# Rotating keys in the stage that makes them, rotating queries straight from PSUM, and four value sums on VectorE

## The chip, the cores and the metric

The kernel runs on one core of a Trainium2 chip. The metric is device time in microseconds (us) for one execution of the whole program; lower is better. In the core, TensorE (PE) multiplies matrices and writes its sums to PSUM banks, VectorE (DVE), ScalarE (ACT) and GpSimd (POOL) work element by element on tiles of 128 partitions, and SyncE (SP) issues most of the DMA transfers. Each engine works through its own instructions in order and waits on semaphores for the others.

## The reference

One sub-layer of an encoder over 1024 tokens of width 1024, in float32. After a root-mean-square norm, one wide projection feeds three mixers: a dilated sliding-window attention ("a", three groups of eight heads of 64, dilations 1, 4 and 16), a grouped-query attention ("b"), and a cross-attention into 256 memory tokens ("m"). Each is gated, projected, and merged by sigmoid gates; an output projection and a norm close it. The change concerns mixer a alone:

```python
def rope(x, pos):
    ang = pos[:, None] * inv[None, :]
    x1, x2 = x[..., :half], x[..., half:]
    return concatenate([x1 * cos - x2 * sin, x1 * sin + x2 * cos], axis=-1)
...
h = rms_norm(x, g_pre)
a_qkv, bq, bk, bv, mq, ga, gb, gm, mg = split(h @ w_in, split_at, axis=-1)
aq = rope(a_qkv[:, :, 0], pos)
ak = rope(a_qkv[:, :, 1], pos)
av = a_qkv[:, :, 2]
for gi, (window, dil) in enumerate(A_GROUPS):
    o_g, lse_g = dilated_window_attention(aq[:, :, hs], ak[:, :, hs], av[:, :, hs], window, dil)
```

A head's rotation needs each feature times a cosine, plus its partner (32 features away in the head of 64) times a sine.

## The kernel before

All of it is one program of some 7,500 matmuls. Activations lie transposed: features on partitions, tokens along the free axis. A float32 product is done as three passes of a faster type: `split` (L105 on ScalarE, L106 on VectorE) cuts an operand into a high part and the rest, and each product is high by high, rest by high, high by rest. A unit of the projection has 128 features; its two halves of 512 tokens take 24 matmuls each into one PSUM bank `d` (L143, L145, L147), and two such banks alternate.

Four stages matter here. The times are those of the profiled execution.

- **Values' stage**, 460 to 598 us. The values of mixer a, and other products of this stage, are computed by a Strassen-Winograd scheme in the order of `PRODUCTS`: A11, A12, S2, S3, S4, S1, A22. `sum_at` forms the weight sums S1 to S4 (all on POOL, L897), `split_at` splits them, `v_out` (L909) adds the last product of a result to what has been kept in `vv` or `vy` and writes it to a tile `vr` (four buffers), and `v_store` scales it on ScalarE and stores it to `vdr`. Beside this `operand` scales the heads of mixer b (tiles `vot`, `vgt`, `vrt`, one buffer each) and stores them back.
- **Keys' stage**, 598 to 714 us. Six blocks `n` of seven products `i`, each product 12 matmuls into a bank `s`. POOL forms four sums in a block (`k_sum`, L978), `k_block` splits them into a tile `ch` (five buffers), and `k_evac` brings a finished product out: into the running sums `kv0` and `kv1` (L1012), or, added to these, into a tile `kr` (`k_out`, L999), which a DMA from ScalarE's queue stores to `kd`. The keys lie in `kd` unrotated, 128 features by 1024 tokens for each of 12 pairs of heads and group.
- **Windowed attention**, 714 to 1106 us. Twelve items (a pair of heads `p_` and a group `g`). `weave` mixes the matmuls of the next query units (`add_a`) on TensorE with the pieces of the attention: scores (L1279, from `aq` and `ak`), the softmax (`soft`: L1291 on VectorE with exponentials on ScalarE, L1292), transposes (L1318), and the products with the values (L1335). Each half of a query unit ends in `q_rope`, and each item's keys are fetched two items ahead by `k_fetch` (step T = 0 of an item) and rotated by `k_rope` (step T = 5).
- From 1106 us on, the merge gates' weights, the branch products and the output projection; the change doesn't touch them.

`q_rope` in the kernel before: VectorE multiplies the bank `d` by the sine table `tab1` into `t3a` (L1182, one buffer) and by the cosine table `tab0` into `t1a` (L1183, two buffers); four DMAs on SP's queue (`swapped`, L1176) move the 32-row quarters of `t3a` to their partners' rows in `t2a`; POOL adds `t1a` and `t2a` into `aq` (L1185), in the order that the group's dilation wants. For the keys, one DMA loads `kraw` from `kd` (L1202), four load `kswp` with quarters exchanged (L1176 too), VectorE multiplies each by a table (L1207, L1208), and POOL subtracts (L1212). The tables are loaded in the second block of the keys' stage and multiplied by the norm's factor `rb` in the third.

In the values' and keys' stages the order on every engine is that of the code. In the attention TensorE's order comes from the costs that `weave` counts; a scheduler sets that of the other engines, except for the first two items' keys, which are again in code order.

Of the kernel before, what the change touches and what calls it, by code (L numbers as in the profile page):

```python
# [15 lines left out]
S = 1024  # L16
# [34 lines left out]
def block(ctx: ExitStack, tc: tile.TileContext, x, xT, memT, cst, msk, bcst, tabA, gpost,  # L51
# [182 lines left out]
    kd = dram.tile([12, P, S], F32, name="kd")  # L234
# [659 lines left out]
    def sum_at(nm, k):  # L894
        a, b, op = {"S1": ("A21", "A22", OP.add), "S3": ("A11", "A21", OP.subtract),
                    "S2": ("S1", "A11", OP.subtract), "S4": ("A12", "S2", OP.subtract)}[nm]
        G.tensor_tensor(VR[nm][:, k], VR[a][:, k], VR[b][:, k], op=op)  # L897
# [9 lines left out]
    def v_out(u, t, j, ps_, z):  # L907
        r = vr()
        V.tensor_tensor(r, ps_, z, op=OP.add)  # L909
# [20 lines left out]
    def operand(r, stage):  # L930
        k, t = r // 2, half[r % 2]
        if stage == 0:
            OT[r] = [vb.tile([P, 512], F32, name=x) for x in ("vot", "vgt", "vrt")]
            nc.sync.dma_start(OT[r][0], od[1, k, :, t])
            nc.sync.dma_start(OT[r][1], g2d[1, k, :, t])
            for h in range(2):
                nc.sync.dma_start(OT[r][2][h * 64:h * 64 + 64], rld[2 * k + h:2 * k + h + 1, t].to_broadcast([64, 512]))
        elif stage == 1:
            ot, gt, rt = OT[r]
            V.scalar_tensor_tensor(ot, ot, 0.5, gt, op0=OP.mult, op1=OP.mult)  # L940
            V.tensor_tensor(ot, ot, rt, op=OP.mult)
        else:
            nc.sync.dma_start(od[1, k, :, t], OT.pop(r)[0])
# [42 lines left out]
    def k_block(n, nm):  # L986
        t = kp.tile([P, 1024], R, name="ch", bufs=5)
# [9 lines left out]
    def k_out(n, u, t, ps_, z):  # L997
        r = kp.tile([P, 512], F32, name="kr", bufs=4)
        V.tensor_tensor(r, ps_, z, op=OP.add)  # L999
        return lambda: nc.scalar.dma_start(kd[2 * n + u, :, half[t]], r)  # L1000

    def k_evac(n, i, ps_):
        nm = PRODUCTS[i][0]
        if nm == "A11":
            return [lambda: A.activation(kv_[0], ps_, AF.Copy)]
        if nm == "A12":
            return [k_out(n, 0, 0, ps_, kv_[0])]
        if nm == "A22":
            return [k_out(n, 1, 0, ps_, kv_[1])]
        if nm == "S1":  # L1010
            return [k_out(n, 1, 1, ps_, kv_[1]), k_out(n, 0, 1, ps_, kv_[0])]
        V.tensor_tensor(kv_[nm == "S3"], ps_, kv_[0], op=OP.add)  # L1012
        return []
# [4 lines left out]
    for n, (i, e, k) in enumerate(steps_v):  # L1018
# [12 lines left out]
        m = n + 2  # L1031
        if m < CLASSIC:
# [13 lines left out]
        for nm, s0 in (("S1", 2), ("S2", 2), ("S3", 7), ("S4", 11)):  # L1046
# [39 lines left out]
    kv_ = [kp.tile([P, 512], F32, name=f"kv{j}") for j in range(2)]  # L1086
    k_sum(0, 3)
# [3 lines left out]
    for n in range(6):  # L1091
        for i, (an, bn) in enumerate(PRODUCTS):
# [7 lines left out]
            behind = left.pop(0)() if left else []  # L1100
            if i == 0:
                k_block(n, "A22")
# [29 lines left out]
            if n == 1 and i == 3:  # L1132
                for j in range(2):
                    nc.sync.dma_start(tab[j], tabA[:, j])
# [5 lines left out]
            left.append(lambda n=n, i=i, b=dst: k_evac(n, i, b))  # L1140
    for f in left.pop(0)():
        f()
# [10 lines left out]
    with tc.tile_pool(name="aa", bufs=1, reuse_waits="tile") as aa:  # L1153
# [19 lines left out]
        def swapped(dst, src):  # L1173

            for a in range(4):
                nc.sync.dma_start(dst[32 * a:32 * a + 32], src[32 * (a ^ 1):32 * (a ^ 1) + 32])  # L1176

        def q_rope(o, half, p, g):

            t = slice(half * 512, half * 512 + 512)  # L1180
            t1, t2, u = [(ab if j == 1 else aa).tile([P, 512], F32, name=f"t{j}a", bufs=2 if j < 3 else 1) for j in (1, 2, 3)]
            V.scalar_tensor_tensor(u, p, -0.125, tab[1][:, t], op0=OP.mult, op1=OP.mult)  # L1182
            fp["last"] = V.scalar_tensor_tensor(t1, p, -0.125, tab[0][:, t], op0=OP.mult, op1=OP.mult)  # L1183
            swapped(t2, u)
# [14 lines left out]
        def k_fetch(p_, g):  # L1199

            KK[p_, g] = [ab.tile([P, S], F32, name=x) for x in ("kraw", "kswp")]
# [3 lines left out]
        def k_rope(p_, g):  # L1205
            kr, ks = KK.pop((p_, g))
            V.tensor_tensor(kr, kr, tab[0], op=OP.mult)  # L1207
            V.tensor_tensor(ks, ks, tab[1], op=OP.mult)  # L1208
            ka = OPS.setdefault((p_, g), {})["k"] = ab.tile([P, S], F32, name="ak", bufs=2)
            for x in range(2):  # L1210
                t = half[x]
                G.tensor_tensor(half_of(ka, x, g), classes(kr[:, t], g), classes(ks[:, t], g), op=OP.subtract)  # L1212
# [172 lines left out]
        def plan(it, pre, nxt):  # L1385
# [18 lines left out]
            def keys(key, T):  # L1404
                if T == 0:
                    k_fetch(*key)
                else:
                    with tc.issue_after(fp["last"].ins):
                        k_rope(*key)
# [7 lines left out]
            for T in range(NT if it else 4):  # L1417
# [7 lines left out]
                if it and it["ahead"] and T in (0, 5):  # L1425
# [115 lines left out]
        def first_keys():  # L1541
            yield 300.0
            k_rope(*seq[0])
            k_fetch(*seq[1])
            yield 400.0
            k_rope(*seq[1])
# [478 lines left out]
```

## Time and profile before

| | before |
|---|---|
| three runs, us | 1549.29, 1545.55, 1548.0 (median 1548.0) |
| profiled execution, us | 1544.46 |
| its span, us | 1542.7 |
| mean granted TensorE clock | 0.971 |
| busy, PE | 1431.0 us, 93% |
| busy, DVE | 937.8 us, 61% |
| busy, ACT | 655.8 us, 43% |
| busy, POOL | 532.1 us, 34% |

How to read it: the profile shows one execution. The span runs from its first instruction to its last, and the device time counts 1.8 us around it. An engine's busy time is the sum over its instructions, so it says little by itself: an engine can be busy for 61% of the span and still hold up another at one place. The granted clock is the share of TensorE's full rate that the chip allowed. A row of a stage gives the time from and to, its length, then busy time and number of instructions of each engine, the clock, the DMA engines' mean busy share, and GB/s. In a row of waits, "A <- B" means that A waited for B, followed by the total in us, the number of waits and the longest. In rows in order of time, the first number is the start in us, the second the duration, and brackets give the wait just before it and what ended it. "L143" is line 143 of the kernel printed above.

### The profile page before, as it was taken

Reading aid. Unit: us, or ns where it says so; the run is one execution under the profiler, and the core shown is the slowest. Engines: PE = TensorE matmul, PEld = TensorE weight load, DVE = VectorE, ACT = ScalarE, POOL = GpSimd, SP = SyncE. Lnnn points to the kernel's source line nnn. Section 1 sums busy time; section 2 is a strip of 40 time slices with the busy share of each in tenths; the row PEclk is TensorE's granted clock in tenths of the full one; section 3 lists DMA queues with packets and bytes.
Section 4 is the critical chain, followed back from the end, with each engine's and each line's share of the span. In section 5 each row is a group of like instructions: output and inputs, shape, how many; then the busy total and the mean of one; then the engine's idle time right before and its main releaser. Section 6 shows DMA issues by size and latency. Waiting matters only on the chain.

```text
span 1542.7 us, 21224 instructions
## 1 busy us (share of the span) xinstructions
PE 1431.0 (93%) x7556; PEld 1144.9 (74%) x7556; DVE 937.8 (61%) x1637; ACT 655.8 (43%) x1407; POOL 532.1 (34%) x406
## 2 busy tenths in 40 slices
PE   7999999999998989998698677787999999999998
PEld 7899876666666868887576565666887788888887
DVE  7755477767636746553434435554478878658743
ACT  6633456656553344221255353545543434222221
POOL 1325307666666003330323332331133333024322
PEclk9999999999999999999899798989999999999999
DMA  6322122222107694334344344433444443757132
GB/s 237 107 86 69 35 89 69 85 90 80 58 23 231 203 279 142 132 117 152 90 119 114 93 128 126 129 87 127 129 140 131 156 165 130 272 190 271 66 110 96
DMA packets 114139, 198.69 MB, mean 129 GB/s; under 512 B 25137, under 2 KB 54897, under 8 KB 114033
## 3 DMA queue, kind: packets, MB, share of 16 engines
q1 hardware_dynamic: 91424, 173.08, 34.9%
q10 hardware_dynamic: 22608, 24.25, 4.5%
q8 instruction: 59, 0.97, 0.3%
q14 instruction: 48, 0.39, 0.1%
HBM read 142.40 MB, written 48.59 MB: 124 GB/s over the span
## 4 chain that ended last, share of the span: by engine, by line
PE 68%; DMA 9%; DVE 9%; ACT 5%; issue 4%; POOL 3%; SPq 2%; ACTq 0%; DVEq 0%; POOLq 0%
PE s L125 15%; PE sc L125 8%; PE d L143 6%; PE d L145 5%; PE d L147 5%; PE sc L1871 4%; PE ov L755 3%; PE s L1029 3%; DMA t2a<-t3a 2%; PE tr L1335 2%; PE s L1279 2%; PE s L739 2%; PE tr L721 2%; PE s L740 2%; DMA wr<-in_wu 2%
## 5 line engine op out<-in xcount | busy, mean ns | idle before, releaser
L143 PE MATMUL d<-hh,wh 128*128 128x512 f32 x480 | 200.8, 418 | 48.6 <-DVE t1a L1183 46.8
L147 PE MATMUL d<-hh,wl 128*128 128x512 f32 x480 | 198.4, 413 | 0.0
L145 PE MATMUL d<-hl,wh 128*128 128x512 f32 x480 | 196.6, 410 | 0.0
L746 POOL TENSOR_TENSOR bl<-bl,bp 128x512 f32<-128x512 f32 x96 | 131.4, 1369 | 53.7 <-ACT bp L742 48.2
L143 PEld LDWEIGHTS d<-hh,wh 128*128 128x128 f32 x480 | 93.7, 195 | 72.3 <-DVE t1a L1183 35.3
L105 ACT ACTIVATE wh<-wr 128x1024 fp32r<-128x1024 f32 (+1 forms) x75 | 67.2, 898 | 170.7 <-PE sc L125 76.0
L125 PE MATMUL sc<-hh,wh 128*128 128x512 f32 x384 | 118.4, 389 | 0.0
L145 PEld LDWEIGHTS d<-hl,wh 128*128 128x128 f32 x480 | 93.9, 196 | 21.8 <-issue 6.3
L147 PEld LDWEIGHTS d<-hh,wl 128*128 128x128 f32 x480 | 93.0, 194 | 22.6 <-issue 5.0
L106 DVE TENSOR_TENSOR wl<-wr,wh 128x1024 fp32r<-128x1024 f32 x47 | 69.4, 1478 | 65.4 <-ACT wh L105 65.2
L1292 ACT ACTIVATE pra<-pra,sts 128x192 f32<-128x192 f32 (+2 forms) x192 | 84.2, 439 | 49.2 <-DVE sts L1291 48.6
L1291 DVE CUSTOM_DVE_ANT_0 pra<-s,mask 128x192 f32<-128x192 f32 (+2 forms) x192 | 56.0, 347 | 78.5 <-PE s L1279 66.9
L1185 POOL TENSOR_TENSOR aq<-t1a,t2a 128x512 f32<-128x512 f32 x24 | 45.0, 1874 | 159.9 <-DMA t2a<-t3a 141.2
L722 DVE TENSOR_REDUCE bn<-tr 128x1 f32<-128x512 f32 x128 | 86.1, 685 | 17.5 <-PE tr L721 16.2
L742 ACT ACTIVATE bp<-s 128x512 f32<-128x512 f32 x128 | 75.8, 595 | 46.6 <-PE s L740 45.5
L106 DVE TENSOR_TENSOR ch<-sf,ch 128x512 fp32r<-128x512 f32 x68 | 58.4, 860 | 42.1 <-ACT ch L105 42.1
L125 PEld LDWEIGHTS sc<-hh,wh 128*128 128x128 f32 x384 | 72.1, 188 | 14.9
L1598 POOL TENSOR_TENSOR sf<-wr 128x512 f32<-128x512 f32 x22 | 31.2, 1437 | 142.5 <-DMA wr<-in_wu 62.1
L1802 POOL TENSOR_TENSOR acc<-acc,th 128x1024 f32<-128x1024 f32 x15 | 40.9, 2728 | 108.8 <-DVE th L1801 106.1
L125 PE MATMUL s<-hh,ch 128*128 128x512 f32 x224 | 74.1, 392 | 1.5 <-ACT ch L105 1.5
L125 PE MATMUL sc<-hl,wh 128*128 128x512 f32 x192 | 74.7, 389 | 0.0
L978 POOL TENSOR_TENSOR sf<-wr 128x512 f32<-128x512 f32 x12 | 20.9, 1745 | 145.3 <-DMA wr<-in_wu 97.9
(384 smaller groups left out, 3724.3 us busy)
## 6 DMA issues: line engine op xcount, KB each, us to landing
wr<-in_wu SPq DMA_DIRECT2D x64, 512.0 KB
th<-thd SPq DMA_DIRECT2D x24, 512.0 KB
thd<-rs ACTq DMA_DIRECT2D x44, 256.0 KB
g2d<-fth SPq DMA_DIRECT2D x24, 256.0 KB
vdr<-vr ACTq DMA_DIRECT2D x24, 256.0 KB
kd<-kr ACTq DMA_DIRECT2D x24, 256.0 KB
kraw<-kd SPq DMA_DIRECT2D x12, 512.0 KB
kswp<-kd SPq DMA_DIRECT2D x48, 128.0 KB
```

Source lines behind the costliest of these rows:

```text
L105: A.activation(dst_h, src, AF.Copy)
L106: V.tensor_tensor(dst_l, src, dst_h.bitcast(F32), op=OP.subtract)
L125: PE.matmul(out_ps, a, b, start=i == 0, stop=i == n - 1)
L143: PE.matmul(dst, wh[:, k, :], hh[k][:, t], start=k == 0, stop=False)
L145: PE.matmul(dst, wh[:, k, :], hl[k][:, t], start=False, stop=False)
L147: PE.matmul(dst, wl[:, k, :], hh[k][:, t], start=False, stop=k == 7)
L722: fp["last"] = V.tensor_reduce(st[i]["n"][:, j, c:c + 1], s, axis=AX.X, op=OP.min)
L742: A.activation(pp, s, AF.Exp, scale=-1.0)
L746: G.tensor_tensor(lsum[i % 2], lsum[i % 2], pp, op=OP.add)
L1291: fp["last"] = V.tensor_tensor_reduce(src, sv[h], mask[:, m0:m0 + n], 1.0, 3.0e38, OP.add, OP.min, bias)
L1292: A.activation(src, src, AF.Exp, scale=-1.0, bias=bias, accum_out=sts[:, h, 1, T:T + 1])
L1871: PE.matmul(parts[h], *terms[h][j], start=j == 0, stop=j == 23)
```

## The change

The diff has three parts.

1. Keys. `kd` has two planes. After `k_out` has a result `r`, a later step (`turn_it`, taken from a list `turns` at products 1, 2, 4 and 6 of a block, 4 and 6 in the first) multiplies it by both tables on VectorE and stores both products. `kr` has six buffers and `ch` four; `k_evac` runs ahead of the product's splits rather than behind them; S2's `ch` is split in the first slot of its own block, not in the sixth of the block before; and the tables are loaded at the start of the stage. In the attention `k_fetch` (step T = 1) loads the cosine product as it is and the sine product with quarters exchanged, and `k_add` (T = 5) has only the sums on POOL, now additions (the sign is in the table).
2. Queries. `t3a` and the DMAs that swapped its quarters are gone. Four operations on 32 partitions each read a quarter of the bank `d` and of the table and write it to its partner's rows of `t2a`; a fifth writes `t1a`.
3. Values. The sums S2 are formed on VectorE, two steps later than before and ahead of that step's split; A22's and S1's results are written in place over `vy` or `vv`; `vot` has two buffers.

```diff
-    kd = dram.tile([12, P, S], F32, name="kd")
+    kd = dram.tile([2, 12, P, S], F32, name="kd")
...
-        G.tensor_tensor(VR[nm][:, k], VR[a][:, k], VR[b][:, k], op=op)
+        (V if nm == "S2" else G).tensor_tensor(VR[nm][:, k], VR[a][:, k], VR[b][:, k], op=op)
...
-    def v_out(u, t, j, ps_, z):
-        r = vr()
+    def v_out(u, t, j, ps_, z, place=False):
+        r = z if place else vr()
...
-            return [v_out(1, 0, j, ps_, vy[j])]
+            return [v_out(1, 0, j, ps_, vy[j], True)]
         if nm == "S1":
-            return [v_out(1, 1, j, ps_, vy[j]), v_out(0, 1, j, ps_, vv[j])]
+            return [v_out(1, 1, j, ps_, vy[j]), v_out(0, 1, j, ps_, vv[j], True)]
...
-            OT[r] = [vb.tile([P, 512], F32, name=x) for x in ("vot", "vgt", "vrt")]
+            OT[r] = [vb.tile([P, 512], F32, name=x, bufs=2 if x == "vot" else 1) for x in ("vot", "vgt", "vrt")]
...
-        t = kp.tile([P, 1024], R, name="ch", bufs=5)
+        t = kp.tile([P, 1024], R, name="ch", bufs=4)
...
-        r = kp.tile([P, 512], F32, name="kr", bufs=4)
+        r = kp.tile([P, 512], F32, name="kr", bufs=6)
         V.tensor_tensor(r, ps_, z, op=OP.add)
-        return lambda: nc.scalar.dma_start(kd[2 * n + u, :, half[t]], r)
+        def turn_it():
+            c = kp.tile([P, 512], F32, name="kr", bufs=6)
+            V.tensor_tensor(c, r, tab[0][:, half[t]], op=OP.mult)
+            V.tensor_tensor(r, r, tab[1][:, half[t]], op=OP.mult)
+            for x, z in enumerate((c, r)):
+                nc.scalar.dma_start(kd[x, 2 * n + u, :, half[t]], z)
+        turns.append(turn_it)
...
+        if 0 <= n - 4 < 4:
+            sum_at("S2", n - 4)
...
-        for nm, s0 in (("S1", 2), ("S2", 2), ("S3", 7), ("S4", 11)):
+        for nm, s0 in (("S1", 2), ("S3", 7), ("S4", 11)):
...
+    for j in range(2):
+        nc.sync.dma_start(tab[j], tabA[:, j])
...
-            behind = left.pop(0)() if left else []
+            if left:
+                k_evac(*left.pop(0))
             if i == 0:
+                if n:
+                    k_block(n, "S2")
                 k_block(n, "A22")
...
-            elif i == 5:
-                k_block(n + 1, "S2")
...
-            if n == 2 and i == 4:
+            if (n, i) == (0, 2):
                 V.tensor_tensor(tab[0], tab[0], rb, op=OP.mult)
                 G.tensor_tensor(tab[1], tab[1], rb, op=OP.mult)
-            for f in behind:
-                f()
+            if i in ((1, 2, 4, 6) if n else (4, 6)) and turns:
+                turns.pop(0)()
...
-            V.scalar_tensor_tensor(u, p, -0.125, tab[1][:, t], op0=OP.mult, op1=OP.mult)
+            for a in range(4):
+                i, j = slice(32 * a, 32 * a + 32), slice(32 * (a ^ 1), 32 * (a ^ 1) + 32)
+                V.scalar_tensor_tensor(t2[i], p[j], -0.125, tab[1][j, t], op0=OP.mult, op1=OP.mult)
             fp["last"] = V.scalar_tensor_tensor(t1, p, -0.125, tab[0][:, t], op0=OP.mult, op1=OP.mult)
-            swapped(t2, u)
...
-            nc.sync.dma_start(KK[p_, g][0], kd[p_ * 3 + g])
-            swapped(KK[p_, g][1], kd[p_ * 3 + g])
+            nc.sync.dma_start(kr, kd[0, p_ * 3 + g])
+            for a in range(4):
+                i, j = slice(32 * a, 32 * a + 32), slice(32 * (a ^ 1), 32 * (a ^ 1) + 32)
+                nc.sync.dma_start(ks[i], kd[1, p_ * 3 + g, j])
...
-            V.tensor_tensor(kr, kr, tab[0], op=OP.mult)
-            V.tensor_tensor(ks, ks, tab[1], op=OP.mult)
...
-                if it and it["ahead"] and T in (0, 5):
+                if it and it["ahead"] and T in (1, 5):
```

How it moves VectorE's instructions in the attention, at the second half of the second query unit. Before, with numbers that tell buffers apart: `d_6865` is that half's bank, `t3a_6892` and `t1a_6890` are its products, and `kraw`, `kswp` are a fetched item's keys.

```order
L1182 SCALAR_TENSOR_TENSOR t3a_6892<-d_6865,tab1_5886 128x512
L1291 ISA pra_7002,sts_6916<-s1_6985,mask_6721 128x256
...
L1291 ISA pra_7029,sts_6916<-s1_6986,mask_6721 128x256
L1291 ISA sts_6916 128x1
L1207 TENSOR_TENSOR kraw_6936<-kraw_6936,tab0_5885 128x1024
L1208 TENSOR_TENSOR kswp_6937<-kswp_6937,tab1_5886 128x1024
L1291 ISA pra_7049,sts_6916<-s1_6991,mask_6721 128x256
...
L1291 ISA sts_6916 128x1
L1183 SCALAR_TENSOR_TENSOR t1a_6890<-d_6865,tab0_5885 128x512
```

And now, where `d_6943` is that half's bank and `d_6906` the one of the half before it:

```order
L1194 SCALAR_TENSOR_TENSOR t2a_6936<-d_6906,tab1_5878 32x512 x4
L1195 SCALAR_TENSOR_TENSOR t1a_6935<-d_6906,tab0_5877 128x512
L1194 SCALAR_TENSOR_TENSOR t2a_6969<-d_6943,tab1_5878 32x512 x2
L106 TENSOR_TENSOR wl_7210<-wr_7207,wh_7209 128x1024
L1194 SCALAR_TENSOR_TENSOR t2a_6969<-d_6943,tab1_5878 32x512
L1302 ISA pra_7007,sts_6992<-s1_6993,mask_6809 128x192
...
L1194 SCALAR_TENSOR_TENSOR t2a_6969<-d_6943,tab1_5878 32x512
L1302 ISA pra_7027,sts_6992<-s1_7000,mask_6809 128x256
...
L1195 SCALAR_TENSOR_TENSOR t1a_6968<-d_6943,tab0_5877 128x512
```

The two table products of the keys have left VectorE's queue, each half has five operations on its bank where it had two, and softmax operations still stand between some of the five.

VectorE in one block of the keys' stage (the second). Before: `sf` are the sums, `ch` the splits' results, `kv` the running sums and `kr` the results.

```order
L106 TENSOR_TENSOR ch_6054<-wr_5936,ch_6054 128x512
L106 TENSOR_TENSOR ch_6073<-sf3_5652,ch_6073 128x512
L999 TENSOR_TENSOR kr_6092<-s1_6060,kv0_5890 128x512
L106 TENSOR_TENSOR ch_6094<-sf0_5649,ch_6094 128x512
L1012 TENSOR_TENSOR kv0_5890<-s1_6079,kv0_5890 128x512
L106 TENSOR_TENSOR wl_6116<-wr_6057,wh_6115 128x1024
L1012 TENSOR_TENSOR kv1_5891<-s1_6098,kv0_5890 128x512
L106 TENSOR_TENSOR ch_6136<-sf2_5651,ch_6136 128x512
```

Now:

```order
L1000 TENSOR_TENSOR kr_6052<-s1_6017,kv1_5883 128x512
L106 TENSOR_TENSOR ch_6054<-sf1_5642,ch_6054 128x512
L106 TENSOR_TENSOR ch_6057<-wr_5931,ch_6057 128x512
L106 TENSOR_TENSOR ch_6076<-sf3_5644,ch_6076 128x512
L1004 TENSOR_TENSOR kr_6081<-kr_6032,tab0_5877 128x512
L1005 TENSOR_TENSOR kr_6032<-kr_6032,tab1_5878 128x512
L1000 TENSOR_TENSOR kr_6099<-s1_6062,kv0_5882 128x512
L106 TENSOR_TENSOR ch_6101<-sf0_5641,ch_6101 128x512
L1004 TENSOR_TENSOR kr_6104<-kr_6052,tab0_5877 128x512
L1005 TENSOR_TENSOR kr_6052<-kr_6052,tab1_5878 128x512
L1024 TENSOR_TENSOR kv0_5882<-s1_6086,kv0_5882 128x512
```

Pairs of table products (L1004, L1005) stand between the splits, and a result is taken out of its bank ahead of the split that it used to follow.

SP's queue where the attention starts. Before:

```order
L1202 DMA kraw<-kd 128x1024
L1176 DMA kswp<-kd 32x1024 x4
L114 DMA wr<-in_wu 128x1024 x3
L1176 DMA t2a<-t3a 32x512
L114 DMA wr<-in_wu 128x1024
L1176 DMA t2a<-t3a 32x512 x3
```

Now:

```order
L1213 DMA kraw<-kd 128x1024
L1216 DMA kswp<-kd 32x1024 x4
L114 DMA wr<-in_wu 128x1024 x4
L1213 DMA kraw<-kd 128x1024
L1216 DMA kswp<-kd 32x1024 x4
```

The loads of weights (`wr`) and of keys are what is left in it; the swaps that stood between them are gone.

More of the change, by code (lines that the diff above doesn't have):

```diff
@@ L1004, in k_evac @@
         if nm == "A11":
[L1005 to L1013, printed above, removed]
+            A.activation(kv_[0], ps_, AF.Copy)
+        elif nm == "A12":
+            k_out(n, 0, 0, ps_, kv_[0])
+        elif nm == "A22":
+            k_out(n, 1, 0, ps_, kv_[1])
+        elif nm == "S1":
+            k_out(n, 1, 1, ps_, kv_[1])
+            k_out(n, 0, 1, ps_, kv_[0])
+        else:
+            V.tensor_tensor(kv_[nm == "S3"], ps_, kv_[0], op=OP.add)
     CLASSIC = 28
@@ L1211, in k_rope @@
                 t = half[x]
[L1212 removed]
+                G.tensor_tensor(half_of(ka, x, g), classes(kr[:, t], g), classes(ks[:, t], g), op=OP.add)
         def item(p_, g):
@@ L1404, in keys @@
             def keys(key, T):
[L1405 to L1409, printed above, removed]
+                (k_fetch if T == 1 else k_add)(*key)
             def ready():
```

25 lines of the change are left out of this document (11 added, 14 removed).

## The prediction

> **What bounds the kernel now.** I read the busy times by stage first (us of the stretch, then busy time and instructions of each engine, the granted clock, the DMA share, GB/s).
>
> ```profile
> core 0: us, PE busy (x) PEld busy (x) DVE busy (x) ACT busy (x) POOL busy (x), PEclk, DMA share, GB/s
> 460.00:598.00 138.00, 127.17 (x540) 102.53 (x539) 84.20 (x111) 54.33 (x92) 32.06 (x20) 0.98 0.69 222
> 598.00:714.00 116.00, 116.00 (x504) 94.41 (x503) 65.10 (x83) 30.71 (x48) 34.50 (x22) 1.00 0.35 122
> 714.00:1106.00 392.00, 312.99 (x2165) 250.75 (x2164) 178.53 (x529) 176.93 (x550) 108.58 (x56) 0.90 0.42 116
> 1106.00:1543.00 437.00, 429.13 (x1908) 354.32 (x1907) 304.95 (x367) 143.21 (x263) 135.82 (x82) 1.00 0.45 158
> ```
>
> TensorE is the bound. In what follows 1106 it works 429 of 437 us; the values' stage (460 to 598) leaves it idle for 10.8, the keys' stage (598 to 714) not at all, and the windowed attention (714 to 1106) for 79 us, at a clock of 0.90. Next the waits of TensorE in the attention (total, times, longest), and who waits for the swap of the queries' rows there.
>
> ```profile
> PE d L143 <- DVE t1a L1183: 46.8, 7, 9.1
> PE s L1279 <- POOL aq L1185: 22.6, 2, 14.5
> ...
>   DVE t3a L1182: 43.3, 12
> ...
> L1176 SPq DMA_DIRECT2D t2a<-t3a x96: 507/588/673, 726.9 to 1057.6; - x96
> ```
>
> Nine waits, 69.4 us, hang on queries: seven on a bank of `d` that `t1a` frees, two on a finished `aq`. The DMA that swaps rows of `t3a` into `t2a`, 96 issues on SP's queue at 0.59 us, holds up VectorE's next `t3a` for 43.3 us, and `aq` can't be summed before it lands. One such wait in order of time:
>
> ```profile
> 750.28 0.69 DVE L1182 SCALAR_TENSOR_TENSOR t3a<-d,tab 128x512 f32<-128x512 f32 x1 [4.20 <-DMA t2a<-t3a]
> 751.72 0.76 PE L143 MATMUL d<-hh,wh 128*128 128x512 f32 x1 [9.07 <-DVE t1a L1183]
> ...
> 754.72 0.39 PE L145 MATMUL d<-hl,wh 128*128 128x512 f32 x1
> ...
> 597.73 116.24 PE s L125 x504
> ```
>
> VectorE can't write the one `t3a` again before the last swap has landed, so `t1a` is late and TensorE stands for 9.07 us. Afterwards it is slow: the eighth matmul of this run starts at 754.72, so seven take 3.0 us, where the keys' stage runs one in 116.24 / 504 = 0.231 us, seven in 1.6. A restart costs 1.4 us more. The Trainium skill ("TensorE: Matmul & The Clock Gate", Part 1) gives about 3.4 us at half rate after a pause, an estimate of 1.7 us per restart; the trace shows 1.4, and by the page the time below would be about 2 us lower.
>
> **The attention, part by part.** The swap goes: `t3a`, 96 DMAs, and both table products of the keys (L1207, L1208). In come four quarter operations (32 rows in, another 32 out) for each of 24 halves, all on VectorE.
>
> ```profile
> L1182 DVE SCALAR_TENSOR_TENSOR t3a<-d,tab 128x512 f32<-128x512 f32 x24 | 16.5, 688 | 52.6 <-DMA t2a<-t3a 43.3 <-PE d L147 4.8 <-PE tr L1335 4.6
> L1207 DVE TENSOR_TENSOR kraw<-kraw,tab 128x1024 f32<-128x1024 f32 x12 | 14.7, 1229 | 7.2 <-DMA kraw<-kd 7.2
> L1208 DVE TENSOR_TENSOR kswp<-kswp,tab 128x1024 f32<-128x1024 f32 x12 | 14.6, 1217 | 0.0
> L675 DVE TENSOR_TENSOR QL<-tr,QH 64x512 fp32r<-64x512 f32 x16 | 11.0, 687 | 8.8 <-ACT QH L672 8.6
> L1627 DVE TENSOR_TENSOR rs<-rs,rb 128x512 f32<-128x512 f32 x44 | 31.2, 709 | 1.5
> ```
>
> No row has 32 partitions; L675 has 64, moves rows between halves in half of its cases, and costs 687 ns like 128. I take 0.69 for a quarter; the bounds are 0.69 and 1.78 (a slow operation shown below). VectorE: 178.5 - 16.5 - 14.7 - 14.6 = 132.7, plus 96 x 0.69 = 66.2, so 199 us: 61% of a shorter stage. A half's five operations take 3.4 us in place of 1.4, and the bank is wanted a whole half later (24 x 0.231 = 5.5 us of matmuls, and attention besides). POOL's sums of `aq` and `ak` keep their form; `aq` loses its DMA. The loads of `kraw` and `kswp` stay, one step later, on an SP queue 96 issues shorter.
>
> The first wait stays and grows:
>
> ```profile
> 719.76 6.89 SPq L114 DMA_DIRECT2D wr<-in_wu  x3
> 727.20 1.22 DVE L106 TENSOR_TENSOR wl<-wr,wh 128x1024 fp32r<-128x1024 f32 x1 [0.32 <-ACT wh L105]
> 729.17 0.76 PE L143 MATMUL d<-hh,wh 128*128 128x512 f32 x1 [4.33 <-DVE t1a L1183]
> ```
>
> SP's weight loads wait for the last stores of keys, and two turns of products (4 x 0.71 = 2.8 us) now come before these. On VectorE the second split of weights (727.20) still stands ahead, now with three quarters and `t1a` behind it in place of `t1a`: 3 x 0.6 = 1.8 us more. I add 5 us (2.8 + 1.8, rounded up; bounds 2 and 8). The other eight waits go: 69.4 - 4.3 = 65.1, with eight restarts at 1.4 = 11.2. What is late next is the attention's own chain; between waits it has held TensorE up little:
>
> ```profile
> 768.58 0.80 PE L143 MATMUL d<-hh,wh 128*128 128x512 f32 x1 [4.77 <-DVE t1a L1183]
> 784.17 0.28 PE L1348 MATMUL tr<-cs,sts 128*32 128x128 f32 x1 [0.43 <-ACT app L1321]
> 806.36 0.44 PE L1318 MATMUL tr<-cs,pra 128*128 128x128 f32 x2 [0.30 <-ACT app L1321]
> 825.70 0.28 PE L1348 MATMUL tr<-cs,sts 128*32 128x128 f32 x1 [0.88 <-ACT app L1321]
> 838.47 0.80 PE L143 MATMUL d<-hh,wh 128*128 128x512 f32 x1 [4.46 <-DVE t1a L1183]
> ```
>
> 1.6 us in 65. The small waits of before stay (79 - 69.4 = 9.6); for five-operation bursts ahead of the softmax I add 5 (bounds 0 and 30). Attention: -65.1 - 11.2 + 5 + 5 = -66.
>
> **The keys' stage.** In: 48 products of 128x512 with both inputs in SBUF, 24 stores more on ACT's queue (6.3 MB, while DMA is busy for 0.35), the tables' load earlier (VectorE waits for it at the third product of the first block), `ch` with four buffers, and S2's split in its own block, 5.5 us before its product. TensorE hides all this while VectorE keeps up. A block is 84 matmuls, 19.4 us:
>
> ```profile
> 617.40:636.80 19.40, 19.40 (x86) 15.79 (x85) 10.05 (x14) 4.78 (x8) 6.08 (x4) 1.00 0.50 176
> ...
> 488.49 6.82 POOL L897 TENSOR_TENSOR vA<-vA,vA 128x512 f32<-128x512 f32 x4
> ...
> 489.00 1.78 DVE L106 TENSOR_TENSOR sl<-sl 128x512 fp32r<-128x512 f32 x1
> ```
>
> 10.05 + 8 x 0.71 = 15.7 us of 19.4 fits. But beside a POOL sum the same kind of operation takes 1.78 in place of some 0.7 (L1627), and a block has 6.08 us of sums: if the products wait out all of it, 21.8, which is 2.4 over, 12 us in five blocks. ACT's stores also wait for their products, and splits queue behind them. Between 0 and 12 I take +5, nearer the fit, since most of a block has no sum.
>
> **The values' stage.**
>
> ```profile
> PE s L1029 <- DVE sl L106: 8.0, 4, 3.7
> PE d L1029 <- DVE vr L909: 2.7, 1, 2.7
> ...
> 549.14 0.69 DVE L909 TENSOR_TENSOR vr<-d,vy 128x512 f32<-128x512 f32 x1 [1.80 <-DMA vdr<-vr]
> 563.83 1.22 PE L1029 MATMUL s<-sl,hh 128*128 128x512 f32 x2 [3.56 <-DVE sl L106]
> ```
>
> Results written in place free `vr` of stores (-2.7); with that and two `vot`, SP reaches the weight load behind the 3.56 sooner. S2 costs VectorE 4 x 0.69 = 2.8 and spares it four sums' company; placed ahead of A12's splits it may cost TensorE 1 to 3. I take -5, bounds -10.7 and +3.
>
> **The sum.** The profiled execution took 1544.46 (span 1542.7): 1544.5 - 66 + 5 - 5 = 1478.5. The runs' median, 1548.0, is 3.5 above it; I say 1480.
>
> **The rivals.** (1) VectorE becomes the keys' bound: all 48 products at 1.78 give 65.1 + 85.4 = 150.5 us for 116, +34 in place of +5: 1509. For: TensorE has no slack there. Against: half the stage has no POOL sum. The Trainium skill ("SBUF — State Buffer", "Who interferes with whom") says a VectorE operation with two SBUF inputs and a GpSimd one that reads SBUF lock each other out whole; the 1.78 agrees, and by it POOL's 34.5 us are the most that can be added: 65.1 + 34 + 34.5 = 133.6, an estimate of 1493. (2) The order of VectorE's queue, not the DMA, holds the banks: before 768.58 and 838.47 softmax and table products stood ahead of `t1a` too. If all eight stay at 4.6 with a restart, 8 x 6.0 = 48 of the 76 us remain, +43: 1523. Against: the table products are gone, and the new order has no score that TensorE issues late ahead of a bank's last operation. (3) Slower: a quarter on shifted partitions is dear. VectorE fills the old 392 us from (392 - 132.7) / 96 = 2.7 us each; at 3.0 it takes 421, +29, 1573. Against: L675.
>
> **Chances.** The forecast (waits gone, keys' stage at most 17 longer: 1460 to 1497) 0.78; (1) 0.10; (2) 0.08; (3) 0.03; no change 0.01. Low end: 1544.5 - 76.3 - 8 = 1460. High end 1512 takes in (1). Within 0.3% of before (about what a measurement here can't tell from no change) needs losses of 60 us at once: 0.02; slower 0.03; faster 0.95.
>
> **What would show it.** In the attention: no t2a DMA, TensorE's waits on `t1a` down to one at the start of some 9 us, none on `aq` over 3, clock above 0.96, the stage near 326 us. Keys: some 121 us, VectorE near 100 busy, any wait of TensorE on `ch`. Values: no wait on `vr`. I am wrong if `t1a` (L1195) still releases TensorE throughout, if quarters take over 1 us, or if TensorE waits tens of us on `ch`.

## The result, and the profile after

| | before | changed |
|---|---|---|
| median of four runs, us | 1548.18 | 1474.7 |
| lowest to highest, us | 1545.55 to 1549.29 | 1471.58 to 1478.09 |
| profiled execution, us | 1544.46 | 1477.48 |

The ratio is 0.9528, with a 95% interval of 0.9498 to 0.9558. The forecast was 1480 for the median and 1478.5 for the profiled execution. The four runs of the changed kernel lie in two pairs, at 1471.6 and 1471.9 (clock 0.995) and at 1477.5 and 1478.1 (clock 0.991); the profile shows one of the upper pair, and what sets the pairs apart no run here tells.

Busy time by stage in the changed kernel (columns as before), each stage from its first matmul to the next stage's (the last row runs 0.4 us past it):

```profile
core 0: us, PE busy (x) PEld busy (x) DVE busy (x) ACT busy (x) POOL busy (x), PEclk, DMA share, GB/s
...
461.70:589.90 128.20, 122.97 (x530) 99.90 (x529) 85.86 (x113) 53.38 (x90) 28.10 (x17) 0.99 0.75 246
589.90:706.12 116.22, 116.22 (x505) 94.59 (x504) 94.83 (x125) 30.18 (x49) 35.95 (x21) 1.00 0.45 157
706.12:1039.00 332.88, 303.16 (x2167) 240.11 (x2166) 207.99 (x583) 173.22 (x551) 102.67 (x56) 0.97 0.42 121
```

The lengths of the stages from one first matmul to the next, read in the same way in every profile (us; the 462 before and the 437 behind these stages are the same in all of them within 2 us):

| kernel | values | keys | attention | median |
|---|---|---|---|---|
| before | 135.6 | 116.2 | 392.0 | 1548.2 |
| changed | 128.1 | 116.2 | 332.5 | 1474.7 |
| e1, queries alone | 137.5 | 116.2 | 361.3 | 1514.1 |
| e2, keys alone | 135.0 | 116.2 | 376.7 | 1536.8 |
| e3, values alone | 129.1 | 116.2 | 390.8 | 1540.7 |
| e4, two t3a | 137.1 | 116.2 | 389.8 | 1542.5 |
| e5, quarters twice | 129.0 | 116.2 | 348.0 | 1494.2 |
| e6, cosine product thrice | 128.3 | 142.4 | 334.5 | 1507.0 |
| e7, S2 on POOL | 127.8 | 116.2 | 329.6 | 1475.2 |
| e8, weights first | 127.8 | 116.2 | 320.2 | 1465.3 |
| e9, turns at the sums | 128.1 | 116.9 | 332.0 | 1478.0 |
| e10, queries, keys' products on POOL | 134.6 | 116.2 | 335.5 | 1488.5 |
| e11, results not in place | 131.9 | 116.2 | 328.9 | 1478.0 |
| e12, e8 and later statistics | 128.9 | 116.2 | 309.6 | 1452.7 |

So 59.5 us came from the attention, 7.5 from the values' stage, none from the keys' stage and none lost there. A difference of a few us between two rows says little: kernels with the same code in the values' stage differ there by up to 1.3 us in the changed form (127.8 to 129.1) and by 2.9 in the old one (134.6 to 137.5), and the attention of the changed kernel, e6, e7, e9 and e11, which is the same code, lies between 328.9 and 334.5. TensorE's waits in the attention of the changed kernel (total, times, longest):

```profile
PE tr L1359 <- ACT app L1332: 12.3, 10, 2.8
PE d L143 <- DVE t1a L1195: 9.8, 1, 9.8
PE tr L1320 <- ACT app L1332: 3.1, 4, 1.3
PE tr L1329 <- ACT app L1332: 2.5, 8, 0.5
PE tr L1320 <- ACT pra L1303: 1.6, 2, 1.0
```

They sum to 29.3 us, against 79 before. Of the seven waits on `t1a` one is left, at the start; those on `aq` are gone. What grew is the waits of transposes for ScalarE's copies `app`, 17.9 us against 8.2; before, the largest of them was

```profile
PE tr L1348 <- ACT app L1321: 6.9, 5, 3.7
```

A quarter costs what a whole operation did:

```profile
L1194 DVE SCALAR_TENSOR_TENSOR t2a<-d,tab 32x512 f32<-32x512 f32 x96 | 66.0, 687 | 56.6 <-PE d L147 54.9
```

### The profile page after: what moved, and what is told of

It is laid out like the page before. It is cut to its first block, busy times and chain, and to the rows that moved or that the text cites. A ratio compares the mean times of both kernels' runs of the same rounds, so it can differ in the third digit from the quotient of the medians.

```text
span 1475.7 us, 21171 instructions
## 1 busy us (share of the span) xinstructions
PE 1419.1 (96%) x7556; PEld 1133.2 (77%) x7556; DVE 998.7 (68%) x1737; ACT 651.6 (44%) x1407; POOL 523.1 (35%) x402
## 3 DMA queue, kind: packets, MB, share of 16 engines
q1 hardware_dynamic: 86816, 166.78, 34.5%
## 4 chain that ended last, share of the span: by engine, by line
PE 68%; DVE 12%; ACT 7%; DMA 5%; issue 4%; POOL 3%; SPq 1%; ACTq 0%; DVEq 0%; POOLq 0%
PE s L125 16%; PE sc L125 9%; PE d L147 6%; PE d L145 6%; PE d L143 5%; PE sc L1878 5%; PE s L1040 4%; PE ov L755 3%; ACT pra L1303 3%; DVE t2a L1194 2%; PE s L739 2%; PE tr L721 2%; PE s L740 2%; PE d L536 2%; DMA wr<-in_wu 1%
## 5 line engine op out<-in xcount | busy, mean ns | idle before, releaser
L143 PE MATMUL d<-hh,wh 128*128 128x512 f32 x480 | 196.6, 410 | 11.5 <-DVE t1a L1195 9.8
L1194 DVE SCALAR_TENSOR_TENSOR t2a<-d,tab 32x512 f32<-32x512 f32 x96 | 66.0, 687 | 56.6 <-PE d L147 54.9
L742 ACT ACTIVATE bp<-s 128x512 f32<-128x512 f32 x128 | 75.9, 595 | 46.8 <-PE s L740 45.7
L105 ACT ACTIVATE ch<-sf 128x512 fp32r<-128x512 f32 x68 | 41.6, 628 | 93.8 <-PE s L125 46.3
L1605 POOL TENSOR_TENSOR sf<-wr 128x512 f32<-128x512 f32 x22 | 30.6, 1409 | 144.2 <-DMA wr<-in_wu 61.4
```

The source lines that it names most:

```text
L105: A.activation(dst_h, src, AF.Copy)
L143: PE.matmul(dst, wh[:, k, :], hh[k][:, t], start=k == 0, stop=False)
L742: A.activation(pp, s, AF.Exp, scale=-1.0)
L1194: V.scalar_tensor_tensor(t2[i], p[j], -0.125, tab[1][j, t], op0=OP.mult, op1=OP.mult)
```

## The experiments

**The three parts alone.** e1 has the five operations of the queries (`q_rope` of the changed kernel in the kernel before):

```diff
-            V.scalar_tensor_tensor(u, p, -0.125, tab[1][:, t], op0=OP.mult, op1=OP.mult)
+            for a in range(4):
...
+                V.scalar_tensor_tensor(t2[i], p[j], -0.125, tab[1][j, t], op0=OP.mult, op1=OP.mult)
-            swapped(t2, u)
```

> The kernel before with the queries' part alone: five operations straight from PSUM, no t3a and no swapping DMAs; keys are still multiplied by the tables on VectorE in the attention (24 operations of 1.2 us), the values' stage is as before. Theory (the one t3a behind its DMA holds the banks): TensorE's waits on t1a and aq go almost whole, the attention falls by 55 to 62 us as in the changed kernel, 1483 to 1490 us. Rival (the order of VectorE's queue holds them, table products and softmax ahead of t1a): with the table products still in that queue half of the 69 us of waits stays, 1505 to 1525 us.

Measured: 1514.1, ratio 0.979 (0.9773 to 0.9806); the attention fell by 30.7 us, half of what the theory said. The rival's number came out, but not with its waits. TensorE's in the attention of e1:

```profile
PE tr L1350 <- ACT app L1323: 31.0, 10, 6.4
PE d L143 <- DVE t1a L1186: 13.7, 2, 7.2
```

The banks wait only twice, near the stage's start; it is the statistics' transpose (L1350 here) that waits. The longest such wait, followed back through VectorE, ScalarE and TensorE:

```profile
834.35 1.22 DVE L1209 TENSOR_TENSOR kraw<-kraw,tab 128x1024 f32<-128x1024 f32 x1
835.49 1.22 DVE L1210 TENSOR_TENSOR kswp<-kswp,tab 128x1024 f32<-128x1024 f32 x1
...
845.07 1.81 DVE L1480 TENSOR_TENSOR ceg<-ceg,cds 128x48 f32<-128x48 f32 x1
...
848.30 1.23 DVE L106 TENSOR_TENSOR wl<-wr,wh 128x1024 fp32r<-128x1024 f32 x1
...
850.29 0.36 DVE L1293 CUSTOM_DVE_ANT_0 pra<-s,mask 128x192 f32<-128x192 f32 x1
...
850.75 0.45 ACT L1294 ACTIVATE pra<-pra,sts 128x192 f32<-128x192 f32 x1 [6.51 <-DVE sts L1293]
...
853.40 0.57 ACT L1323 ACTIVATE app<-tr 128x512 f32<-128x512 f32 x1
...
854.02 0.39 PE L1350 MATMUL tr<-cs,sts 128*32 128x128 f32 x1 [6.37 <-ACT app L1323]
```

From 834.35 on VectorE has in its queue, almost without a pause, the keys' products (2.4 us), the end of a softmax, the operations that weigh the groups' results (L1469 to L1480, 5.3 us), eight of the ten operations of two halves (5.5 us) and a split of weights, and only at 850.29 the next item's softmax. ScalarE waits 6.5 us for that, then does six exponentials ahead of the copy that frees the bank. TensorE is held by a copy, and what made the copy late is VectorE's queue. This wait alone doesn't tell how much of it is due to the keys' products; e10 below does.

e2 has the keys' part alone, the queries as before.

```diff
-    kd = dram.tile([12, P, S], F32, name="kd")
+    kd = dram.tile([2, 12, P, S], F32, name="kd")
...
-            V.tensor_tensor(kr, kr, tab[0], op=OP.mult)
-            V.tensor_tensor(ks, ks, tab[1], op=OP.mult)
```

> The kernel before with the keys' part alone: both products made and stored in the keys' stage, only sums in the attention; queries keep t3a, the four DMAs and their wait. Theory: the keys' stage costs TensorE nothing, and in the attention VectorE still waits some 43 us for the swaps, so 1535 to 1550 us, about as before. Rival (order of VectorE's queue): 29.3 us of table products gone from it shorten the waits by a third to a half, 1510 to 1530 us.

Measured: 1536.8, ratio 0.9925 (0.9895 to 0.9955). The time lies in the theory's range. Yet the attention fell by 15.3 us in the profile, where the theory had nothing and the rival a third to a half of the waits. The profiled execution took 1528.7, 8 us less than the median, so 15.3 is rather too much; by medians the whole gain is 11.3. TensorE's waits on `t1a` stayed at 47.7 us in eight; the one on `aq` fell to 7.3:

```profile
PE d L143 <- DVE t1a L1195: 47.7, 8, 8.8
PE s L1291 <- POOL aq L1197: 7.3, 1, 7.3
```

e3 has the values' part alone (the diff's lines on `sum_at`, `v_out` and `vot`).

> The kernel before with the values' part alone: S2 on VectorE two steps later, results in place, two vot. Theory: the values' stage becomes 7 to 8 us shorter as in the changed kernel and nothing else moves, 1539 to 1541 us. Rival (the earlier end is eaten in the next stages, whose transfers then come late): no change, 1546 to 1549 us.

Measured: 1540.7, ratio 0.9959 (0.9944 to 0.9973), the values' stage 6.5 us shorter: as the theory said, but for half a us in the stage. The three parts alone give 34.0 + 11.3 + 7.4 = 52.7 us of medians, all together 73.5. The missing 20.8 lie mostly in the attention: 30.7 + 15.3 = 46.0 alone in the profiles, 59.5 together.

**Is it the one buffer?** e4 gives the kernel before two buffers of `t3a`, with one less of `app` to make room.

```diff
-            t1, t2, u = [(ab if j == 1 else aa).tile([P, 512], F32, name=f"t{j}a", bufs=2 if j < 3 else 1) for j in (1, 2, 3)]
+            t1, t2, u = [(ab if j == 1 else aa).tile([P, 512], F32, name=f"t{j}a", bufs=2) for j in (1, 2, 3)]
...
-                pp = aa.tile([P, 4, 128], F32, name="app", bufs=6)
+                pp = aa.tile([P, 4, 128], F32, name="app", bufs=5)
```

> The kernel before with two buffers of t3a in place of one (the tile app has five in place of six, to make room). The swapping DMAs, their landing and the number of VectorE operations stay. Theory: VectorE's 43 us of waits for a free t3a fall under 10, TensorE's 47 us on t1a fall under 15, while the two waits on aq (22.6 us) stay, as the landing is what they wait for: 1500 to 1515 us. Rival (VectorE's order, or the queue of DMAs itself, sets the pace, and a second buffer only moves the wait): within 1535 to 1550 us.

Measured: 1542.5, ratio 0.9968 (0.9951 to 0.9985), the rival's range. The waits on `t1a` did fall, from 46.8 to 9.3, and VectorE's own for a free `t3a` from 43.3 to 23.5, where the theory had under 10; but those on `aq`, which waits for the same DMAs to land, rose from 22.6 to 49.4, and those on copies from 6.9 to 15.5:

```profile
PE s L1279 <- POOL aq L1185: 49.4, 4, 15.6
PE tr L1348 <- ACT app L1321: 15.5, 7, 2.9
PE d L143 <- DVE t1a L1183: 9.3, 2, 4.7
```

So the single buffer only chose which of the swap's waiters held TensorE. The stage became 2.2 us shorter, not the 33 to 48 of the theory. For the two longest of the four waits on `aq`, 15.3 us up to 893.0 and 15.6 up to 979.2, SP's queue shows why the swaps were late. Around the first it has

```profile
858.14 0.60 SPq L1176 DMA_DIRECT2D t2a<-t3a  x1
...
884.64 11.50 SPq L1176 DMA_DIRECT2D t2a<-t3a  x15
```

and other loads and stores between: the swaps stood behind these in the queue. Whether they would have been in time on another engine's queue was not tried. Nor is e4 the second buffer alone: with five buffers of `app`, ScalarE's copies waited 44.1 us for the products that read it (L1335), a wait that the kernel before doesn't have.

**Is it the products' place in VectorE's queue?** e10 is e1 with the keys' 24 products on POOL.

```diff
-            V.tensor_tensor(kr, kr, tab[0], op=OP.mult)
-            V.tensor_tensor(ks, ks, tab[1], op=OP.mult)
+            G.tensor_tensor(kr, kr, tab[0], op=OP.mult)
+            G.tensor_tensor(ks, ks, tab[1], op=OP.mult)
```

> The kernel before with the queries' part (as in e1, 361.3 us of attention) and the keys' 24 table products of 128x1024 moved from VectorE to POOL at the same place, some 65 us more there. Theory (in e1 the products stand in VectorE's queue ahead of softmax and queries' operations, and that is the 29 us by which it misses the changed kernel): the attention comes down to 333 to 345 us, 1486 to 1500 us. Rival (the products are late by themselves, through the loads of keys ahead of them, and ak with them; or POOL, slower, takes their part): 361 us or more, 1514 or above.

Measured: 1488.5, ratio 0.9619 (0.9601 to 0.9638), the attention at 335.5: the theory's number, and 25.8 of the 28.8 us between e1 and the changed kernel are back, at the price of 60 us of POOL's time, which stood idle.

```profile
L1210 POOL TENSOR_TENSOR kswp<-kswp,tab 128x1024 f32<-128x1024 f32 x12 | 30.4, 2537 | 5.3 <-DMA kswp<-kd 5.3
L1209 POOL TENSOR_TENSOR kraw<-kraw,tab 128x1024 f32<-128x1024 f32 x12 | 29.5, 2459 | 33.1 <-DMA kraw<-kd 33.1
```

And TensorE's largest wait in that stage:

```profile
PE tr L1350 <- ACT app L1323: 16.3, 10, 2.8
```

The statistics' waits went from 31.0 to 16.3, and the longest from 6.4 to 2.8. With the swap gone, the products cost what they did because VectorE had to do them; that their place ahead of the softmax is what counts is read from the waits of e1.

**How much room has VectorE in the attention?** e5 issues each quarter twice, the second over the first.

```diff
                 V.scalar_tensor_tensor(t2[i], p[j], -0.125, tab[1][j, t], op0=OP.mult, op1=OP.mult)
+                V.scalar_tensor_tensor(t2[i], p[j], -0.125, tab[1][j, t], op0=OP.mult, op1=OP.mult)
```

> The changed kernel with every quarter operation of the queries issued twice: 96 more of 0.69 us, 66 us more on VectorE in the attention, 208 + 66 = 274 us of 333. Theory (what is left in the attention is VectorE's delay of the softmax, seen as TensorE's waits on app): those waits grow from 18 to 35 or more, with restarts 20 to 35 us, 1493 to 1510 us. Rival (VectorE has room, and each bank is free long before it is wanted): at most 5 us, 1472 to 1480 us.

Measured: 1494.2, at the lower edge of the theory's range, but 15.5 us in the attention for 65 us of work, where the theory had 20 to 35 and the rival at most 5. The waits on `app`, 28.5 us in all, stayed under the theory's 35. Both kinds of wait grew, the copies' and the first one:

```profile
PE tr L1360 <- ACT app L1333: 22.0, 10, 5.1
PE d L143 <- DVE t1a L1196: 14.0, 2, 12.8
```

VectorE is busier here than in e1, 273 us against 248, and the stage is 13 us shorter. That speaks for the place of the work in the queue rather than its amount.

**How much room in the keys' stage?** e6 issues the cosine product of each turn three times, into the same tile.

```diff
             V.tensor_tensor(c, r, tab[0][:, half[t]], op=OP.mult)
+            V.tensor_tensor(c, r, tab[0][:, half[t]], op=OP.mult)
+            V.tensor_tensor(c, r, tab[0][:, half[t]], op=OP.mult)
```

> The changed kernel with the cosine product of each turn issued three times: 48 more operations of 0.68 us, 32.8 us more on VectorE in the keys' stage, 94.8 + 32.8 = 127.6 us where the stage has 116.2. Theory (TensorE hides VectorE's work up to its own 116 us and no further): the stage becomes 8 to 14 us longer, with TensorE waiting on ch, 1480 to 1488 us. Rival (VectorE already holds up TensorE there at 95 us busy, since products stand ahead of splits): 25 to 33 us longer. If it stays within 3 us of the changed kernel, the work has run over into the attention's first microseconds.

Measured: 1507.0, and the stage 26.2 us longer for 32.8 us of work: the rival's number. TensorE stood idle for 16.2 us of it, and its 504 matmuls took 10 us longer, at a granted clock of 0.93. The stage's row:

```profile
590.29:732.68 142.39, 126.17 (x505) 99.77 (x504) 125.29 (x166) 29.70 (x49) 35.55 (x21) 0.93 0.36 128
```

What TensorE waited for in e6 (15.8 of the 17.4 us fall in this stage), and what ScalarE waited for in this stage:

```profile
PE s L125 <- ACT ch L105: 17.4, 8, 4.4
...
ACT ch L105 <- DVE kr L1007: 60.3, 8, 9.8
```

In the changed kernel VectorE's wait for ScalarE's copies stands beside its 94.8 us of work:

```profile
L106 DVE TENSOR_TENSOR ch<-sf,ch 128x512 fp32r<-128x512 f32 x24 | 19.0, 796 | 19.5 <-ACT ch L105 19.4
```

VectorE is busy for 94.8 of 116.2 us, which looks like 21 us of room. But ScalarE's queue holds each turn's stores ahead of the next copies, the stores wait for VectorE's products (60.3 us here), and VectorE's splits wait for the copies: work added to a turn passes through all three. In the changed kernel the copies of `ch` show no such wait for products. The loop is read from these waits; the stores on another queue were not tried. VectorE's work inside the stage rose by 125.3 - 94.8 = 30.5 us (the last turns fall behind its end), the stage by 26.2: the room was 4.3 us.

**POOL's sums beside the products.** e9 moves the turns to the slots where POOL's sums run.

```diff
-            if i in ((1, 2, 4, 6) if n else (4, 6)) and turns:
+            if i in ((3, 4, 5, 6) if n else (4, 6)) and turns:
```

> The changed kernel with the table products of the keys' stage in slots 3, 4, 5 and 6 of a block instead of 1, 2, 4 and 6, so that they meet POOL's sums, which are issued in slots 3 and 4. Theory (a VectorE operation with both inputs in SBUF is slowed by a POOL sum): the products beside sums take 1.2 to 1.8 us, the sums get longer too, VectorE's busy time in the stage goes from 94.8 to 102 to 112 us, and TensorE loses 0 to 10 us there. Rival (no such lock; the long operations seen elsewhere have another cause): all products stay at 0.68 to 0.69 us, no change.

Measured: 1478.0, the same within what these runs tell apart. VectorE's busy time in the stage, over 116.2 us, was 96.41 instead of 94.91. The cosine products and the splits of e9:

```profile
L1004 DVE TENSOR_TENSOR kr<-kr,tab 128x512 f32<-128x512 f32 x21 | 18.7, 891 | 0.0
...
L106 DVE TENSOR_TENSOR ch<-sf,ch 128x512 fp32r<-128x512 f32 x24 | 17.4, 730 | 23.1 <-ACT ch L105 23.1
```

Sine and cosine products of the changed kernel:

```profile
L1005 DVE TENSOR_TENSOR kr<-kr,tab 128x512 f32<-128x512 f32 x21 | 18.4, 877 | 0.7
...
L1004 DVE TENSOR_TENSOR kr<-kr,tab 128x512 f32<-128x512 f32 x22 | 15.0, 682 | 0.0
```

Products beside sums do get longer (the cosine's mean is 0.89 in place of 0.68 us), but the splits got away from the sums (`ch` from 0.796 to 0.730 us). The slowing is real, and it falls on whatever VectorE does while a sum runs; moving the products there added 1.5 us in all. The theory's direction held, its size didn't.

**Which part of the values' change?** e7 puts S2 back on POOL at its old steps.

```diff
-        (V if nm == "S2" else G).tensor_tensor(VR[nm][:, k], VR[a][:, k], VR[b][:, k], op=op)
+        G.tensor_tensor(VR[nm][:, k], VR[a][:, k], VR[b][:, k], op=op)
...
-        for nm, s0 in (("S1", 2), ("S3", 7), ("S4", 11)):
+        for nm, s0 in (("S1", 2), ("S2", 2), ("S3", 7), ("S4", 11)):
```

> The changed kernel with the sums S2 on POOL again, at their old steps; results in place and two vot stay. Theory: S2 on VectorE takes POOL's slow sums from beside VectorE's splits and is worth about half of the stage's 7.5 us, so the values' stage goes from 128.1 to 131 to 133 us, 1476 to 1480 us. Rival (the free vr and vot did it all): 128 to 129 us, no change in total.

Measured: 1475.2 (1472.5 to 1479.4), the stage at 127.8: the rival. S2 on VectorE did nothing that shows. e11 writes the results to `vr` again.

```diff
-            return [v_out(1, 0, j, ps_, vy[j], True)]
+            return [v_out(1, 0, j, ps_, vy[j])]
...
-            return [v_out(1, 1, j, ps_, vy[j]), v_out(0, 1, j, ps_, vv[j], True)]
+            return [v_out(1, 1, j, ps_, vy[j]), v_out(0, 1, j, ps_, vv[j])]
```

> The changed kernel with A22's and S1's results of the values' stage written to a tile vr again (four buffers), as before the change; S2 on VectorE and two vot stay. Theory (VectorE's wait for a free vr held the bank and the loads behind it, and in place it goes): the stage goes from 128.1 back to 132 to 136 us, 1478 to 1483 us. Rival (the second vot did it, by freeing SP's queue for the weight loads): 128 to 129 us, no change.

Measured: 1478.0 (1476.9 to 1478.9), the stage at 131.9, at the theory's lower edge: writing in place is worth some 3.8 of the 7.5 us, outside the spread of 1.3 us but not far. VectorE's wait for a free `vr` is back (3.0 us in two), and TensorE's waits on the splits `sl` are 6.0 us against 4.3. The stage in e7:

```profile
461.79:589.61 127.82, 123.52 (x530) 100.77 (x529) 82.77 (x109) 53.58 (x90) 33.90 (x21) 0.97 0.75 247
```

And in e11:

```profile
461.95:593.88 131.93, 124.66 (x529) 100.92 (x528) 86.59 (x113) 53.39 (x90) 28.42 (x17) 0.97 0.73 239
```

The other 3.7 us are left for the second `vot`, by subtraction; it was not run by itself.

**Two waits that were left.** The first wait of the attention in the changed kernel, on SP's queue, VectorE and TensorE:

```profile
709.41 0.33 SPq L1213 DMA_DIRECT2D kraw<-kd  x1
709.85 2.01 SPq L1216 DMA_DIRECT2D kswp<-kd  x4
712.01 12.37 SPq L114 DMA_DIRECT2D wr<-in_wu  x4
...
720.83 1.23 DVE L106 TENSOR_TENSOR wl<-wr,wh 128x1024 fp32r<-128x1024 f32 x1 [10.30 <-ACT wh L105]
722.08 0.68 DVE L1194 SCALAR_TENSOR_TENSOR t2a<-d,tab 32x512 f32<-32x512 f32 x1
...
727.00 0.77 PE L143 MATMUL d<-hh,wh 128*128 128x512 f32 x1 [9.82 <-DVE t1a L1195]
```

The second unit's weights are loaded behind the fetch of keys, and the first bank's quarters stand behind their split, though that bank was full, by an estimate, 24 matmuls of 0.231 us after the stage's start, at 711.7. e8 loads these weights first.

```diff
         manual.__enter__()
+        prepare(done[0] + 1)
         k_fetch(*seq[0])
```

> The changed kernel with one line more: the second query unit's weights are loaded and split (prepare) ahead of the fetch of the first keys, so that on SP's queue that load no longer stands behind the fetch's five DMAs, and on VectorE its split stands ahead of the last table products. Theory (TensorE's first wait, 9.8 us on t1a, is the late weight load, behind which VectorE's first quarters stand in the queue): the wait falls under 2 us and its restart goes, the attention 332.5 to 320 to 324 us, 1463 to 1468 us. Rival (the load is held up by the stores of keys before it, wherever it is issued): the wait stays at 7 to 10 us, no change.

Measured: 1465.3 (1464.4 to 1466.7), ratio to before 0.9468 (0.9451 to 0.9484), as the theory said; the attention lost 12.3 us in the profiles, and the wait isn't there. VectorE now has the first four quarters where the bank is full:

```profile
706.45 1.22 DVE L106 TENSOR_TENSOR wl<-wr,wh 128x1024 fp32r<-128x1024 f32 x1
...
711.76 2.79 DVE L1194 SCALAR_TENSOR_TENSOR t2a<-d,tab 32x512 f32<-32x512 f32 x4 [0.24 <-PE d L147]
```

e12 adds a later place for the statistics' transpose, by a larger blank cost ahead of it in the plan.

```diff
-                    out += [(lambda: None, 300.0), pre["stats"]]
+                    out += [(lambda: None, 2500.0), pre["stats"]]
```

> The kernel of e8, and in the plan of an item the blank cost ahead of the statistics' transpose (L1359) is 2500 in place of 300, so that some ten more of the queries' matmuls run before it. Theory (that transpose comes while ScalarE still copies the bank it needs, behind six exponentials that VectorE's burst made late; TensorE has other work that could stand there): its waits fall from 13.2 to under 5 us, 1455 to 1461 us. Rival (the delay is VectorE's, and a later transpose only moves the wait to the pieces behind it or to the matmuls of queries at an item's end): no change from e8, 1463 to 1468 us, with the waits on app under other lines.

Measured: 1452.7 (1450.5 to 1454.6), ratio to before 0.9382 (0.9368 to 0.9397), better than expected. TensorE's waits in the attention of e8:

```profile
PE tr L1359 <- ACT app L1332: 13.2, 10, 2.8
PE tr L1329 <- ACT app L1332: 4.1, 8, 2.2
```

And of e12, with the stage's row:

```profile
PE tr L1329 <- ACT app L1332: 7.5, 7, 2.2
...
PE tr L1359 <- ACT app L1332: 0.9, 1, 0.9
```

```profile
706.81:1016.45 309.64, 296.83 (x2165) 235.96 (x2163) 209.62 (x583) 171.18 (x549) 102.08 (x55) 0.99 0.45 132
```

A few us moved to L1329, and the attention, at 309.6 us with TensorE busy for 296.8, has 12.8 us of idle time left. This version beats both kernels.

## Why the prediction was right, point by point

- **The attention, -66; measured -59.5.** The swap's waits went as forecast (79 to 29.3 us of waits in all). The first wait was forecast at 4.3 + 5 = 9.3 and is 9.8, by the mechanism named: counted from the stage's start, the weights are copied 3.4 us later (forecast 2.8), and from VectorE's second split to `t1a` it takes 2.2 us more (forecast 1.8). The restarts, 11.2, show as TensorE's busy time in the stage falling by 313.0 - 302.8 = 10.2. The Trainium skill's page "TensorE: Matmul & The Clock Gate" (Part 1) would make that, by an estimate of 1.7 each, 8 x 1.7 = 13.6; the trace gives less. The mis-sized term is "5 (bounds 0 and 30)" for the softmax behind the bursts: the small waits went from 9.6 to 19.5, so 10. These three, 5 + 1 + 0.5, are about what is missing.
- **The quarter at 0.69.** It is 0.687, and VectorE in the stage is at 208 us, forecast 199. That settles the third rival.
- **Its reason for the waits was too narrow.** "VectorE can't write the one `t3a` again" is what the row said, but with two of them (e4) the time stayed, as the wait moved to `aq`. Taking the whole swap away ended both. The second rival, the order of VectorE's queue, was argued away with "the table products are gone": e1 and e10 show that this clause carried 25.8 us, for which the sum has no term. Without the keys' part the queries' part would have given half, and the sum came out since both were in the change.
- **The keys' stage, +5 of 0 to 12; measured 0.** The fit of 15.7 in 19.4 us held. But the margin that this sum shows, 3.7 us a block or 22 in six, was 4.3 in the whole stage (e6). The sentence "ACT's stores also wait for their products, and splits queue behind them" names the cause that the waits of e6 point to, and nothing was charged for it; in this change nothing was due.
- **The first rival, VectorE bound by POOL's sums.** 43 of the 48 products fall inside the stage. They take 18.4 + 15.0 = 33.4 us, where 43 x 0.69 = 29.7 is the fast rate: the sums cost them 3.7 us, not the rival's 1.1 us for each product. The Trainium skill's "SBUF — State Buffer" ("Who interferes with whom") has the two engines lock each other out; single operations bear that out (1.67 us beside a sum, 0.69 without). The estimate of 34.5 us more that was made from it did not come: only four products met a sum, one in each of four blocks, as this one beside the sums that POOL starts at 657.95 and 659.70:

```profile
658.51 1.67 DVE L1005 TENSOR_TENSOR kr<-kr,tab 128x512 f32<-128x512 f32 x1
```

- **The values' stage, -5; measured -7.5.** No wait on `vr` is left, which is worth some 3.8 us. S2 costs VectorE 3.1 us more than in e7 (85.86 against 82.77; 2.8 were forecast), and the stage neither gains nor loses by it.

That the sum, -66 forecast and -67.0 in the profiled executions, is nearer than its terms is luck: the attention fell short by 6.5, the keys' stage gave 5 and the values' 2.5 more. By medians the fall was 73.5, where 68 was forecast.

## What to carry to other kernels

When a wait names a buffer, ask what fills the buffer's slow consumer: a second buffer can move the wait to the next reader of the same transfer, while taking the transfer away ends it. On an engine that serves several chains, count what stands ahead of the short, urgent operations in its queue, not its busy share: 35 us of products ahead of a softmax (in e1) cost some 26 us with VectorE 69% busy, and the same products on an idle engine at most 3. Idle time of an engine that waits for another which waits for it is no room; double the work there once and see how much passes through.

## What the runs showed that was not expected

- An operation on 32 partitions that reads PSUM and writes 32 other partitions takes as long as one on 128: 0.687 against 0.688 us for 512 elements. In a row they follow each other more slowly, as VectorE's rows in order of time show for the changed kernel (start, time of the group, and at its end the number in it):

```profile
703.53 1.29 DVE L1000 TENSOR_TENSOR kr<-s,kv 128x512 f32<-128x512 f32 x2 [2.10 <-PE s L125]
...
726.88 2.79 DVE L1194 SCALAR_TENSOR_TENSOR t2a<-d,tab 32x512 f32<-32x512 f32 x4
```

  Two operations on 128 partitions take 1.29 us, so the second starts 0.61 after the first; four quarters take 2.79, 0.70 apart. The Trainium skill ("VectorE: DVE Perf Modes", "Two Vector instructions with no wait between them") says that an operation whose operands start in another group of 32 partitions than the one before starts only when that has finished; the 0.70, the length of one, agrees. It doesn't single this rule out: in e5 the second of two like quarters, on the same groups, starts 0.72 after the first too, though there it writes over the first one's result and may wait for that.
- 24 products of 128x1024 cost some 26 us on VectorE in this stage (e1) and 3 or less on POOL (e10), where each takes longer: 2.46 and 2.54 us against 1.61 and 1.31.
